# One seam pattern instead of thirteen in the feed-forward blocks of a two-layer encoder

## The chip, the cores and the metric

The kernel runs on one core of one Trainium2 chip. The metric is the device time of one launch in microseconds (us). The kernel before takes 1655.82 us in the median of three launches (1652.97 to 1657.56 us). Beside the launches there is one profiled execution of it, and all rows below are from that one.

## What is computed

The reference has two layers. In each layer the 256 tokens of 1024 channels go through a SwiGLU feed-forward network (FFN), a mixer of three attention-like branches, and a second FFN, each followed by a layer norm:

```python
def swiglu(x, w_in, w_out):
    gate, up = jnp.split(x @ w_in, 2, axis=-1)
    return (jax.nn.silu(gate) * up) @ w_out

for l in range(DEPTH):          # DEPTH = 2
    x = layer_norm(alpha * x + 0.5 * swiglu(x, w_ff1_in[l], w_ff1_out[l]), ln1_g[l], ln1_b[l])
    mix = hybrid_mixer(x, ...)
    x = layer_norm(alpha * x + mix, ln2_g[l], ln2_b[l])
    x = layer_norm(alpha * x + 0.5 * swiglu(x, w_ff2_in[l], w_ff2_out[l]), ln3_g[l], ln3_b[l])
```

So there are four FFNs, numbered 0 to 3 here. `w_in` is 1024 x 8192 (4096 gate and 4096 up channels) and `w_out` 4096 x 1024.

## The kernel before

Every float32 operand is split in two parts, `hi` and `lo`, and a product is made of three matmuls: hi x hi, hi x lo and lo x hi. ScalarE makes `hi` (line 90) and VectorE makes `lo` (line 91) of each weight tile of 128 x 1024, which the SyncE queue loads into a ring of three `raw` buffers; `hi` and `lo` have five buffers each.

An FFN works through 32 units of 128 hidden channels (loop in `ffn`, line 291). For one unit, `wide` (line 224) makes gate and up: 2 outputs x 8 slices of the input channels x 3 products = 48 matmuls of 256 columns. They all go through `mm` (line 191) and stand in the profile as line 198. This text calls them *input matmuls*, and writes w for one. After every second unit, `block` (line 203) makes the share of the output that the two units before the newest two give: 2 units x 2 halves of the tokens x 3 products x 2 halves of the output = 24 matmuls of 512 columns, which accumulate over the whole FFN in four PSUM tiles `acc` and stand as line 219. These are *output matmuls*, B for one. A *seam* is the passage from a block's output matmuls to the next unit's input matmuls. TensorE's stream in an FFN is thus, over and over, 24 B and 96 w: one *period*. An FFN has 13 blocks; the last is followed by 192 w, and then `finish` (line 240, matmuls of line 238) adds the last six units with their own weights.

The kernel before doesn't pass every seam in the same way. It keeps back the last few B of a block and puts them between the first w of the next unit. `block` puts them into `self.held`, each with the number of w after which it is due; `mm` counts the w in `self.done` and issues what is due (line 221 in the profile). Which B are kept back is a matter of the seam's *form*, an entry of the table at line 113:

```python
FORMS = ((), (2, 2), (1, 1), (3, 3), (1,), (2,), (3,), (2, 2, 2), (2, 2, 2, 2), (3,) * 6, (3, 6), "first", "rows")
```

The form (2, 2) keeps back two B and issues both after two w; (3, 6) issues one after three w and one after six; () keeps back none. "first" keeps back none but halves the first w into two matmuls of 128 columns (line 195), and "rows" halves the last B into two of 256 columns (line 217). Block j of FFN number f takes entry (j + 3 f) modulo 13, so each FFN passes through all 13 forms once, each time at another place. A seam is where the form's name applies: the form of block j shapes the end of that block and the start of the run of w behind it.

The instructions are laid out by a scheduler which keeps the order within an engine mostly as written. At the start of FFN 1, 2 and 3 it mixes the first block with the layer norm's transposes and the first three units, so that this block stands in pieces. The other 49 seams (13 in FFN 0, 12 in each of the others) stand as written.

Of the kernel before, what the change touches and what calls it, by code (L numbers as in the profile page):

```python
# [77 lines left out]
class Ring:  # L78
    def __init__(self, nc, pool):
        self.nc = nc  # L80
        self.pool = pool
# [28 lines left out]
PGT = ("vv", "vv", "vg")  # L110
PBR = ("vv", "vv", "vg")
ORDER = "K0 G4 B0 K1 G5 C0 K2 B1 K3 G7 k V0 G8 G6 V1 C1 G9 v i s G10 B2 C2 G11 G0 B3 G1 Z0 G2 Z1 G3 p R1 R2 R0"
FORMS = ((), (2, 2), (1, 1), (3, 3), (1,), (2,), (3,), (2, 2, 2), (2, 2, 2, 2), (3,) * 6, (3, 6), "first", "rows")


class Build:
    def __init__(self, nc, tc, pool, psum, dram, a):
        self.nc, self.tc, self.pool, self.psum, self.a = nc, tc, pool, psum, a
        self.ring = Ring(nc, pool)
        self.held, self.done, self.halves, self.nffn = [], 0, False, 0  # L120
        self.con = pool.tile([128, NCONST], F32, name="con")
        self.sums = pool.tile([128, NSUM], F32R, name="sums")
        self.nh = pool.tile([128, 16], F32, name="nh")
        nc.vector.memset(self.nh, -0.5)
        self.en = pool.tile([128, 8], F32, name="en")
        nc.vector.memset(self.en, float(np.e))
        self.dram = [dram.tile([8, 128, 16], F32, tag=f"d{i}", name=f"d{i}") for i in range(3)]
        self.ident = self.con[:, C_ID:C_ID + 128]
        self.xx = pool.tile([128, 8, 2, S], F32R, name="xhl")
        self.xh, self.xl = self.xx[:, :, 0], self.xx[:, :, 1]  # L130
        self.xs = [[x[:, k] for k in range(8)] for x in (self.xh, self.xl)]
        self.x = pool.tile([128, 2, D], F32, name="x")
# [52 lines left out]
    def mm3(self, out, wh, wl, xh, xl, start, stop):  # L185
        mm = self.mm
        mm(out, wh, xh, start=start, stop=False)
        mm(out, wh, xl, start=False, stop=False)
        mm(out, wl, xh, start=False, stop=stop)

    def mm(self, out, w, x, start, stop):
        mm = self.nc.tensor.matmul
        if self.halves:
            for c in (slice(0, 128), slice(128, 256)):
                mm(out[:, c], w, x[:, c], start=start and c.start == 0, stop=stop)
            self.halves = False
        else:
            mm(out, w, x, start=start, stop=stop)  # L198
        self.done += 1
        while self.held and self.held[0][0] <= self.done:  # L200
            self.held.pop(0)[1]()

    def block(self, acc, gs, ws, start, form):
        mm = self.nc.tensor.matmul
        todo = []
        for i, (g, w) in enumerate(zip(gs, ws)):
            for t in range(2):
                c = slice(t * 128, t * 128 + 128)
                for p, (x, y) in enumerate(((g[0], w[0]), (g[0], w[1]), (g[1], w[0]))):
                    for h in range(2):  # L210
                        todo.append((acc[t][h], x[:, c], y[:, h * 512:h * 512 + 512], start and i == 0 and p == 0))
        after = form if isinstance(form, tuple) else ()
        n = len(todo) - len(after)
        for q, (o, x, y, st) in enumerate(todo[:n]):
            if form == "rows" and q == n - 1:
                for d in (slice(0, 256), slice(256, 512)):
                    mm(o[:, d], x, y[:, d], start=st, stop=False)
            else:
                mm(o, x, y, start=st, stop=False)  # L219
        self.done = 0  # L220
        self.held = [(a, lambda o=o, x=x, y=y, st=st: mm(o, x, y, start=st, stop=False)) for a, (o, x, y, st) in zip(after, todo[n:])]  # L221
        self.halves = form == "first"

    def wide(self, out, w, xh, xl, nk):
        n = 0
# [25 lines left out]
    def ffn(self, wi, wo, lnp, first, last):  # L251
        nc = self.nc
        if not first:
            lng = self.load_ln(lnp)
        acc = None
        g = []

        def gate(gg, gate, up):
            s = self.tl(list(gg.shape), "cv")
            nc.scalar.activation(out=s, in_=gate, func=AF.Silu)  # L260
            nc.vector.tensor_tensor(out=gg, in0=s, in1=up, op=ALU.mult)  # L261

        n0 = 2 if first else NFIRST
        if first:
            ps = self.first(wi)
            for u in range(2):
                gg = self.tl([128, S], "th")
                gate(gg, ps[2 * u], ps[2 * u + 1])
                t = self.tl([128, 2, S], "g", F32R)
                self.split(t[:, 0], t[:, 1], gg)  # L270
                g.append((t[:, 0], t[:, 1]))
        else:
            tags = (OTHER + (RING,) * 4)[:2 * n0]
            ws, ps = [], []
            for u in range(n0):
                ws.append(self.ring.chunk(wi[u], tags=tags[2 * u:2 * u + 2], engs=self.engs(PFF[2 * u:2 * u + 2])))
                ps.append(self.ps([128, 2, S], "acc" if u < 2 else "mm"))
                g.append(self.tl([128, 2, S], "g", F32R))
            for t in range(2):
                c = slice(t * 128, t * 128 + 128)  # L280
                for u in range(n0):
                    for k in range(8):
                        hi, lo = [w[:, (k % 4) * S:(k % 4) * S + S] for w in ws[u][k // 4]]
                        self.mm3r(ps[u][:, t], self.xs[0][k][:, c], self.xs[1][k][:, c], hi, lo, k == 0, k == 7)
                    gg = self.tl([128, 128], "th")
                    gate(gg, ps[u][:, t, 0:128], ps[u][:, t, 128:256])
                    tp = self.ps([128, 128], "sm")
                    nc.tensor.transpose(tp, gg, self.ident)
                    self.split(g[u][:, 0, c], g[u][:, 1, c], tp)
            g = [(t[:, 0], t[:, 1]) for t in g]  # L290
        for u in range(n0, 32):
            w = self.ring.chunk(wi[u])
            if first and u in (6, 10):
                with self.tc.issue_after(self.ring.last.ins):
                    if u == 6:
                        self.second()
                    else:
                        lng = self.load_ln(lnp, nc.sync)
            gg = self.tl([128, S], "th")
            ps = self.ps([128, 2, S], ("mm", "sm")[u // 2 % 2])  # L300
            self.wide(ps, w, self.xs[0], self.xs[1], 8)
            gate(gg, ps[:, 0], ps[:, 1])
            t = self.tl([128, 2, S], "g", F32R)
            self.split(t[:, 0], t[:, 1], gg)
            g.append((t[:, 0], t[:, 1]))
            j = u // 2 - 1
            if u % 2 == 1 and u >= 3 and 2 * j < 32 - NLAST:
                if acc is None:
                    acc = [[self.ps([128, 512], "acc") for h in range(2)] for t in range(2)]
                self.block(acc, g[2 * j:2 * j + 2], self.ring.chunk(wo[j]), j == 0, FORMS[(j + 3 * self.nffn) % len(FORMS)])  # L310
        self.nffn += 1
        tags = (EXTRA + (RING,) * 4)[:NLAST]
        ws = []
        for n in range(NLAST // 2):
            ws += self.ring.chunk(wo[16 - NLAST // 2 + n], tags=tags[2 * n:2 * n + 2])
        self.finish(acc, g[32 - NLAST:], ws, 0.5, lng, last)
# [51 lines left out]
    def mixer(self, l):  # L368
# [472 lines left out]
        for j in range(4):  # L841
# [6 lines left out]
            st=2, mv=2, ve=2, rs=2, nm=4, sum=4, rsum=4, es=4)  # L848
# [78 lines left out]
```

## Time and profile before

| | |
|---|---|
| three launches, median | 1655.82 us (1652.97 to 1657.56) |
| profiled execution, its own time | 1655.71 us |
| its span, first to last instruction | 1653.9 us |
| mean granted TensorE clock | 0.997 of full speed |
| TensorE (PE) busy | 1630.6 us, 99% of the span |
| VectorE (DVE) busy | 1046.1 us, 63% |
| ScalarE (ACT) busy | 791.4 us, 48% |
| PE's share of the chain that ended last | 91%; lines 198: 56%, 219: 16%, 238: 8%, 221: 1% |

The profile gives each engine's busy time, the instructions behind it by source line, and what ended each wait. A matmul's busy time overlaps its neighbours' (the end is modelled), so how fast matmuls follow each other is read from their number in a stretch of time and not from the mean duration of one. In a table of windows a number in brackets counts every instruction that touches the window, so two or three at the edges come on top of those that start in it.

### The profile page before, as it was taken

The numbers are of one execution on the slowest core, as the hardware profiler recorded it, in microseconds if no ns is written. First come the engines' busy times: TensorE is split into PE (matmuls) and PEld (weight loads), VectorE is DVE, ScalarE is ACT, GpSimd is POOL, SyncE is SP. The second block draws the span as 40 slices with busy tenths as digits, with TensorE's granted clock in tenths as the row PEclk, the third lists the DMA queues.
The fourth block names the chain that finished last, engine by engine and source line by source line (L and its number), as shares of the span: only waits on it lengthen the run. The fifth ranks groups of instructions, "written<-read, shape, count | busy, mean of one in ns | idle before, by whom it ended". The sixth has DMA issues, their size and how long they took to land.

```text
span 1653.9 us, 29281 instructions
## 1 busy us (share of the span) xinstructions
PE 1630.6 (99%) x12246; PEld 1521.2 (92%) x12246; DVE 1046.1 (63%) x1580; ACT 791.4 (48%) x1297; POOL 175.1 (11%) x145
## 2 busy tenths in 40 slices
PE   9999999999999999999999999999999999999998
PEld 7999998999889899999999999989988889999997
DVE  6555555889669755555655555667886696555555
ACT  5444453675444444444444444536754444444442
POOL 0000001123014400000110000011320152000000
PEclk9999999999999999999999999999999999999999
DMA  8655553634335555555555555535353355555552
GB/s 319 226 198 181 198 203 120 222 141 154 129 131 195 182 201 183 199 181 201 184 199 185 197 183 199 198 137 208 139 164 120 108 202 180 204 199 185 195 185 77
DMA packets 52341, 298.28 MB, mean 180 GB/s; under 512 B 11600, under 2 KB 13520, under 8 KB 18672
## 3 DMA queue, kind: packets, MB, share of 16 engines
q1 hardware_dynamic: 50208, 289.39, 48.9%
q0 software_dynamic: 2000, 7.01, 1.2%
q8 instruction: 96, 1.57, 0.4%
q14 instruction: 37, 0.30, 0.1%
HBM read 294.94 MB, written 1.44 MB: 179 GB/s over the span
## 4 chain that ended last, share of the span: by engine, by line
PE 91%; DVE 5%; DMA 1%; ACT 1%; issue 1%; SPq 0%; POOL 0%; DVEq 0%; ACTq 0%; POOLq 0%
PE mm L198 36%; PE sm L198 20%; PE acc L219 16%; PE acc L238 8%; DVE lo L91 2%; PE acc L221 1%; DMA raw<-w1i 1%; PE acc L322 1%; PE acc L320 1%; PE acc L704 1%; PE acc L321 1%; PE sm L534 1%; PE sm L585 1%; ACT hi L90 1%; PE sm L526 1%; DVE cv L478 1%
## 5 line engine op out<-in xcount | busy, mean ns | idle before, releaser
L91 DVE TENSOR_TENSOR lo<-raw,hi 128x1024 fp32r<-128x1024 f32 (+1 forms) x498 | 617.4, 1245 | 481.7 <-ACT hi L90 480.8
L90 ACT ACTIVATE hi<-raw 128x1024 fp32r<-128x1024 f32 (+1 forms) x542 | 564.2, 1050 | 656.8 <-PE mm L198 196.0
L198 PE MATMUL mm<-xhl,hi 128*128 128x256 f32 x3486 | 619.6, 280 | 0.0
L198 PEld LDWEIGHTS mm<-xhl,hi 128*128 128x128 f32 x3486 | 533.8, 188 | 9.0 <-issue 5.8
L198 PE MATMUL mm<-xhl,lo 128*128 128x256 f32 x1744 | 487.7, 280 | 0.0
L198 PE MATMUL sm<-xhl,hi 128*128 128x256 f32 x1950 | 341.5, 279 | 0.8 <-ACT hi L90 0.8
L198 PEld LDWEIGHTS mm<-xhl,lo 128*128 128x128 f32 x1744 | 330.0, 189 | 3.7 <-issue 2.4
L198 PEld LDWEIGHTS sm<-xhl,hi 128*128 128x128 f32 x1950 | 298.4, 188 | 3.4 <-ACT hi L90 1.0
L198 PE MATMUL sm<-xhl,lo 128*128 128x256 f32 x976 | 271.9, 279 | 0.8 <-DVE lo L91 0.8
L219 PE MATMUL acc<-hi,g 128*128 128x512 f32 x752 | 209.5, 390 | 0.0
L198 PEld LDWEIGHTS sm<-xhl,lo 128*128 128x128 f32 x976 | 184.6, 189 | 1.4 <-DVE lo L91 1.0
L219 PEld LDWEIGHTS acc<-hi,g 128*128 128x128 f32 x752 | 137.0, 188 | 25.1
L91 POOL TENSOR_TENSOR lo<-raw,hi 128x1024 fp32r<-128x1024 f32 (+1 forms) x44 | 103.8, 2373 | 368.8 <-DVE g L147 243.8
L219 PE MATMUL acc<-lo,g 128*128 128x512 f32 x396 | 122.4, 389 | 0.0
L343 POOL TENSOR_TENSOR rs<-ve,nh 128x1 f32<-128x1 f32 x12 | 11.8, 982 | 775.0 <-DVE ve L341 775.0
L238 PE MATMUL acc<-hi,g 128*128 128x512 f32 x320 | 92.8, 392 | 0.0
L219 PEld LDWEIGHTS acc<-lo,g 128*128 128x128 f32 x396 | 74.3, 188 | 15.8
L238 PEld LDWEIGHTS acc<-hi,g 128*128 128x128 f32 x320 | 59.3, 188 | 13.3 <-DVE g L149 0.7
L238 PE MATMUL acc<-lo,g 128*128 128x512 f32 x160 | 54.6, 390 | 0.0
L147 DVE TENSOR_TENSOR g<-th,g 128x256 fp32r<-128x256 f32 x119 | 51.0, 429 | 2.1 <-ACT g L145 1.9
L145 ACT ACTIVATE g<-th 128x256 fp32r<-128x256 f32 x119 | 47.8, 402 | 5.7 <-DVE th L261 5.7
L478 DVE SCALAR_TENSOR_TENSOR cv<-cin,par,cv 128x256 f32<-128x256 f32 x72 | 41.7, 625 | 0.2
(239 smaller groups left out, 1543.5 us busy)
## 6 DMA issues: line engine op xcount, KB each, us to landing
raw<-w2i SPq DMA_DIRECT2D x64, 1024.0 KB, 4.8
raw<-w1i SPq DMA_DIRECT2D x62, 1024.0 KB, 4.8
raw<-w1o SPq DMA_DIRECT2D x32, 1024.0 KB, 4.8
raw<-w2o SPq DMA_DIRECT2D x32, 1024.0 KB, 4.8
raw<-wg SPq DMA_DIRECT2D x28, 1024.0 KB, 4.8
raw<-wgt SPq DMA_DIRECT2D x24, 1024.0 KB, 4.8
raw<-wbr SPq DMA_DIRECT2D x12, 1024.0 KB, 4.8
raw<-wout SPq DMA_DIRECT2D x8, 1024.0 KB, 4.9
```

The source lines that it names most:

```text
L90: nc.scalar.activation(out=hi, in_=raw, func=AF.Copy)
L91: (eng or nc.vector).tensor_tensor(out=lo, in0=raw, in1=hi.bitcast(F32), op=ALU.subtract)
L145: nc.scalar.activation(out=hi, in_=src, func=AF.Copy, scale=scale)
L147: nc.vector.tensor_tensor(out=lo, in0=src, in1=hi.bitcast(F32), op=ALU.subtract)
L198: mm(out, w, x, start=start, stop=stop)
L219: mm(o, x, y, start=st, stop=False)
L221: self.held = [(a, lambda o=o, x=x, y=y, st=st: mm(o, x, y, start=st, stop=False)) for a, (o, x, y, st) in zip(after, todo[n:])]
L238: mm(acc[h], x[:, c], y[:, h * n:h * n + n], start=start and i == 0, stop=stop and i == 2)
L320: mm(out, xh, wh, start=start, stop=False)
L321: mm(out, xh, wl, start=False, stop=False)
L322: mm(out, xl, wh, start=False, stop=stop)
L478: V.scalar_tensor_tensor(out=cv, in0=cin[:, q:q + S], scalar=w[:, q:q + 1], in1=cv, op0=ALU.mult, op1=ALU.add)
```

## The change

The table of forms goes away, and with it the two halving forms and the counter of w. `block` now always keeps back its last two B, and `mm` issues whatever is held right after the next w. That is the form (1, 1) at every seam: 22 B, one w, two B, and then the other w.

```diff
-FORMS = ((), (2, 2), (1, 1), (3, 3), (1,), (2,), (3,), (2, 2, 2), (2, 2, 2, 2), (3,) * 6, (3, 6), "first", "rows")
...
     def mm(self, out, w, x, start, stop):
-        mm = self.nc.tensor.matmul
-        if self.halves:
-            for c in (slice(0, 128), slice(128, 256)):
-                mm(out[:, c], w, x[:, c], start=start and c.start == 0, stop=stop)
-            self.halves = False
-        else:
-            mm(out, w, x, start=start, stop=stop)
-        self.done += 1
-        while self.held and self.held[0][0] <= self.done:
-            self.held.pop(0)[1]()
+        self.nc.tensor.matmul(out, w, x, start=start, stop=stop)
+        held, self.held = self.held, []
+        for h in held:
+            self.nc.tensor.matmul(*h[:3], start=h[3], stop=False)
...
-        after = form if isinstance(form, tuple) else ()
-        n = len(todo) - len(after)
...
+        self.held = todo[-2:]
+        for o, x, y, st in todo[:-2]:
+            self.nc.tensor.matmul(o, x, y, start=st, stop=False)
```

Of the 49 seams that stand as written, four have the form (1, 1) already, one in each FFN; the other 45 change. The pieces of the first blocks of FFN 1, 2 and 3 stand as they did. On VectorE, ScalarE, GpSimd and SyncE the instructions stand in the same order as before, all of them; TensorE loses eight instructions (the second halves) of 11,847 and keeps all others.

TensorE at the first seam of FFN 0, before (form ()): `acc<-hi,g` and `acc<-lo,g` are output matmuls, `xhl,hi` and `xhl,lo` input matmuls of the next unit.

```order
L219 MATMUL acc<-lo,g 128x512 x2
L219 MATMUL acc<-hi,g 128x512 x4
L219 MATMUL acc<-lo,g 128x512 x2
L219 MATMUL acc<-hi,g 128x512 x2
L198 MATMUL mm<-xhl,hi 128x256 x2
L198 MATMUL mm<-xhl,lo 128x256
```

TensorE at the same place after; line 192 is the issue of the held matmuls, line 189 an input matmul.

```order
L204 MATMUL acc<-lo,g 128x512 x2
L204 MATMUL acc<-hi,g 128x512 x4
L204 MATMUL acc<-lo,g 128x512 x2
L189 MATMUL mm<-xhl,hi 128x256
L192 MATMUL acc<-hi,g 128x512 x2
L189 MATMUL mm<-xhl,hi 128x256
L189 MATMUL mm<-xhl,lo 128x256
```

The last two output matmuls moved behind the first input matmul; nothing else moved.

TensorE at the tenth seam of FFN 0, before (form (3,) * 6).

```order
L219 MATMUL acc<-hi,g 128x512 x4
L219 MATMUL acc<-lo,g 128x512 x2
L219 MATMUL acc<-hi,g 128x512 x2
L198 MATMUL sm<-xhl,hi 128x256 x2
L198 MATMUL sm<-xhl,lo 128x256
L221 MATMUL acc<-hi,g 128x512 x2
L221 MATMUL acc<-lo,g 128x512 x2
L221 MATMUL acc<-hi,g 128x512 x2
L198 MATMUL sm<-xhl,hi 128x256 x2
```

TensorE at the same place after.

```order
L204 MATMUL acc<-hi,g 128x512 x4
L204 MATMUL acc<-lo,g 128x512 x2
L189 MATMUL sm<-xhl,hi 128x256
L192 MATMUL acc<-hi,g 128x512 x2
L189 MATMUL sm<-xhl,hi 128x256
L189 MATMUL sm<-xhl,lo 128x256
```

Six output matmuls stood behind three input matmuls; now two stand behind one.

TensorE at the first seam of FFN 1 that stands as written (block 1, form (1,)), before.

```order
L219 MATMUL acc<-hi,g 128x512 x4
L219 MATMUL acc<-lo,g 128x512 x2
L219 MATMUL acc<-hi,g 128x512
L198 MATMUL sm<-xhl,hi 128x256
L221 MATMUL acc<-hi,g 128x512
L198 MATMUL sm<-xhl,hi 128x256
L198 MATMUL sm<-xhl,lo 128x256
```

TensorE at the same place after.

```order
L204 MATMUL acc<-hi,g 128x512 x4
L204 MATMUL acc<-lo,g 128x512 x2
L189 MATMUL sm<-xhl,hi 128x256
L192 MATMUL acc<-hi,g 128x512 x2
L189 MATMUL sm<-xhl,hi 128x256
L189 MATMUL sm<-xhl,lo 128x256
```

One more output matmul moved behind the first input matmul.

## Rows read from the trace of the kernel before

**Rows 1.** The page's first part: engine, busy us, share of the span, instructions.

```profile
PE   1630.6 (99%) x12246; PEld 1521.2 (92%) x12246; DVE 1046.1 (63%) x1580; ACT 791.4 (48%) x1297; POOL 175.1 (11%) x145
```

**Rows 2.** Windows of PE, line 198, one behind each seam of FFN 0, in order.

```profile
core 0: us, PE busy (x), PEclk, DMA share, GB/s
36.80:46.80 10.00, 10.00 (x87) 1.00 0.91 359
54.00:64.00 10.00, 10.00 (x91) 1.00 0.57 210
70.20:80.20 10.00, 10.00 (x90) 1.00 0.72 261
87.00:97.00 10.00, 10.00 (x87) 1.00 0.56 206
103.50:113.50 10.00, 10.00 (x88) 1.00 0.58 211
120.30:130.30 10.00, 10.00 (x87) 1.00 0.55 211
137.10:147.10 10.00, 10.00 (x87) 1.00 0.60 212
154.00:164.00 10.00, 10.00 (x91) 1.00 0.60 211
170.70:180.70 10.00, 10.00 (x87) 1.00 0.53 205
187.40:197.40 10.00, 10.00 (x88) 1.00 0.56 208
204.20:214.20 10.00, 10.00 (x87) 1.00 0.53 208
220.50:230.50 10.00, 10.00 (x91) 1.00 0.59 211
237.00:247.00 10.00, 10.00 (x91) 1.00 0.70 250
```

**Rows 3.** Windows of PE, line 198, in FFN 1, 2 and 3.

```profile
590.50:598.50 8.00, 8.00 (x70) 1.00 0.79 305
788.00:798.00 10.00, 10.00 (x90) 1.00 0.70 256
860.50:868.50 8.00, 8.00 (x73) 1.00 0.71 264
875.00:885.00 10.00, 10.00 (x91) 1.00 0.61 210
1007.60:1017.60 10.00, 10.00 (x91) 1.00 0.61 211
1507.70:1517.70 10.00, 10.00 (x91) 1.00 0.61 211
```

**Rows 4.** Windows of PE, all lines, from a block's first B to a later block's.

```profile
31.19:258.06 226.87, 226.87 (x1661) 1.00 0.58 210
598.76:808.91 210.15, 210.15 (x1540) 1.00 0.55 196
868.93:1079.47 210.54, 210.54 (x1541) 1.00 0.55 195
1418.91:1629.50 210.59, 210.59 (x1540) 1.00 0.53 185
64.30:80.67 16.37, 16.37 (x123) 1.00 0.74 257
97.43:114.19 16.76, 16.76 (x123) 1.00 0.52 189
781.67:808.91 27.24, 27.24 (x218) 1.00 0.65 234
```

**Rows 5.** Groups by line, FFN 0: count, busy us, mean ns, idle before, who ended it.

```profile
L91 DVE TENSOR_TENSOR lo<-raw,hi 128x1024 fp32r<-128x1024 f32 (+1 forms) x87 | 105.4, 1216 | 102.9 <-ACT hi L90 102.9
L90 ACT ACTIVATE hi<-raw 128x1024 fp32r<-128x1024 f32 (+1 forms) x86 | 90.2, 1053 | 117.2 <-issue 37.5 <-PE sm L198 30.2 <-PE mm L198 27.4
```

More of the change, by code (lines that the diff above doesn't have):

```diff
@@ L119, in __init__ @@
         self.ring = Ring(nc, pool)
-        self.held, self.done, self.halves, self.nffn = [], 0, False, 0
+        self.held = []
         self.con = pool.tile([128, NCONST], F32, name="con")
@@ L191, in mm, with block @@
     def mm(self, out, w, x, start, stop):
-        mm = self.nc.tensor.matmul
-        if self.halves:
-            for c in (slice(0, 128), slice(128, 256)):
-                mm(out[:, c], w, x[:, c], start=start and c.start == 0, stop=stop)
-            self.halves = False
-        else:
-            mm(out, w, x, start=start, stop=stop)
-        self.done += 1
-        while self.held and self.held[0][0] <= self.done:
-            self.held.pop(0)[1]()
-    def block(self, acc, gs, ws, start, form):
-        mm = self.nc.tensor.matmul
+        self.nc.tensor.matmul(out, w, x, start=start, stop=stop)
+        held, self.held = self.held, []
+        for h in held:
+            self.nc.tensor.matmul(*h[:3], start=h[3], stop=False)
+    def block(self, acc, gs, ws, start):
         todo = []
@@ L211, in block @@
                         todo.append((acc[t][h], x[:, c], y[:, h * 512:h * 512 + 512], start and i == 0 and p == 0))
-        after = form if isinstance(form, tuple) else ()
-        n = len(todo) - len(after)
[L214 to L222, printed above, removed]
+        self.held = todo[-2:]
+        for o, x, y, st in todo[:-2]:
+            self.nc.tensor.matmul(o, x, y, start=st, stop=False)
     def wide(self, out, w, xh, xl, nk):
@@ L309, in ffn @@
                     acc = [[self.ps([128, 512], "acc") for h in range(2)] for t in range(2)]
-                self.block(acc, g[2 * j:2 * j + 2], self.ring.chunk(wo[j]), j == 0, FORMS[(j + 3 * self.nffn) % len(FORMS)])
-        self.nffn += 1
+                self.block(acc, g[2 * j:2 * j + 2], self.ring.chunk(wo[j]), j == 0)
         tags = (EXTRA + (RING,) * 4)[:NLAST]
```

## The prediction

> **What bounds the kernel now.** The page comes first: TensorE is busy 99% of the span, VectorE 63%, ScalarE 48% [rows 1]. Such a kernel gets faster only if TensorE has less to do or does the same at a closer pace, and the busy share can't show the second, since matmuls overlap in it. So the next view is a table of windows of equal length, one behind each seam of FFN 0, in which the input matmuls are counted [rows 2]. The reader is to see two values there and nothing between: 90 or 91 matmuls of 256 columns in 10 us, or 87 or 88. The granted clock is 1.00 in both, the engine is busy for the whole 10.00 us in both. So there are two paces of the same instruction, about 4% apart, each held for the whole run between two blocks.
>
> The 13 rows of [rows 2] stand behind the 13 forms of the table in order. The close pace (90, 91) follows (2, 2), (1, 1), (2, 2, 2), "first" and "rows"; the wide pace (87, 88) follows (), (3, 3), (1,), (2,), (3,), (2, 2, 2, 2), (3,) * 6 and (3, 6). Hence the reading on which the forecast rests: the form of a seam sets the pace of the run behind it.
>
> A place in the FFN could do that as well as a form, and [rows 3] tells the two apart, because the forms are shifted by three from one FFN to the next. Form (1, 1) stands behind block 2 of FFN 0, 12 of FFN 1, 9 of FFN 2 and 6 of FFN 3, and the windows behind them (third row of [rows 2]; those from 788.00, 1007.60 and 1507.70 in [rows 3]) count 90, 90, 91 and 91: close, four of four. Does the pace ahead of a block matter for the pace behind it? Form (2, 2, 2) answers: in FFN 0 it follows a wide run (87, window from 137.10) and a close run comes (91); in FFN 2 it follows a close run (73 in 8 us, from 860.50, where the wide pace gives 70, as from 590.50) and a close run comes again (91, from 875.00). It was the same behind either.
>
> **The change part by part.** Prices first, by windows from one block's first output matmul to a later one's [rows 4]. A period of 24 B and 96 w takes 16.37 us with form (1, 1), 64.30 to 80.67, and 16.76 us with form (1,), 97.43 to 114.19: 0.39 us for the pace. The long run behind the last block takes 27.24 us with form (1, 1), 781.67 to 808.91.
>
> The 45 seams that change. I replace every period by one of form (1, 1). FFN 0 holds 12 periods and a long run: 12 x 16.37 + 27.24 = 223.68 us for 226.87, a gain of 3.19. The others hold, from the first whole block on, 11 periods and a long run: 11 x 16.37 + 27.24 = 207.31. FFN 1 takes 210.15 (gain 2.84), FFN 2 210.54 (3.23), FFN 3 210.59 (3.28). The sum is 12.54 us. A second way to it: by the list above 8, 7, 7 and 7 of the runs in these stretches are wide, 29 in all, of which two (the ends of FFN 2 and 3) are long runs of 192 w and count about double, so 31 x 0.39 = 12.1; the rest is a little more than the halved matmuls cost.
>
> The eight matmuls less (second halves of "first" and "rows") are in these sums. Alone they are small either way: the same columns are still streamed.
>
> The bookkeeping in Python issues nothing. The order on the other engines is unchanged, so no DMA, no conversion and no queue is passed by another; no wait is added.
>
> What is late next. The weights for 24 w (one tile of 1024 columns, 8 slices by 3 products) are converted by ScalarE in 1.053 us and by VectorE in 1.216 us, one tile behind the other on separate engines [rows 5]. At the close pace TensorE needs 24 x 10/88 = 2.7 us for them (88 being 91 less the three at a window's edges). Of VectorE's idle time all ends with ScalarE, and half of ScalarE's with TensorE, which hands back a buffer. The suppliers wait for the consumer, so a pace 2.4% closer by period (16.37 for 16.76) finds them ready, and I cost this at nothing. If that cover were gone, the price would be bounded by what is gained, 0.39 us per period. The DMA share in the close runs is 0.57 to 0.72, so loads have room as well.
>
> Two things the trace doesn't show. One is form (1, 1) behind a wide run: all four of its seams follow a close one, and with the change the first whole blocks of FFN 1 and 3 do follow a wide one (70 in 8 us from 590.50 for FFN 1; FFN 3 begins with the same pieces). At best it costs 16.37, at worst it keeps 16.76; I take 16.37, for (2, 2) and (2, 2, 2) both turn wide into close. The other is what the mixers do between the FFNs: their order is unchanged and the finish with its matmuls of 512 columns lies before them, so I take 0.
>
> A rule that speaks against the gain. What the rows show: at a granted clock of 1.00, 87 or 91 matmuls of one shape in 10 us [rows 2]. The Trainium skill, page "TensorE: Matmul & The Clock Gate", section "Back-to-back issue gap", gives the warm distance of isolated matmuls by the columns alone, N/2.4 + 2.5 ns, thus 109 ns for 256 columns wherever they stand. By that rule the order can't matter and the sum would be 0; by the rows it is 12.5 us. The trace disagrees, with one shape at two paces, and I go by the trace.
>
> The sum: 1655.71 us of the profiled execution (its span of 1653.9 and 1.8 around it) less 12.5 is 1643.2. The median of the launches is 1655.82, the same within 0.1.
>
> **The rivals.** *The seam hands on the pace that it meets.* Form (1, 1) would keep a close run close and a wide run wide. For it: all four of its seams have close on both sides. Against it: its neighbour (2, 2) always turns wide to close, and (2, 2, 2) gave one outcome behind either pace. FFN 0 and 2 begin close and would gain 3.19 + 3.23; FFN 1 and 3 would be wide throughout: 11 x 16.76 and a long run of 27.24 + 2 x 0.39 = 28.02 (estimate) make 212.38, a loss of 2.23 and 1.79. Time: 1655.7 - 6.42 + 4.02 = 1653.3.
>
> *The pace belongs to the place or to the instruction stream as a whole*, and forms only happen to go with it, or the supply of weights can't hold the close pace for 160 us on end. Nothing is gained: 1655.7. Against it: the four places of (1, 1) in [rows 2, 3], and the end of FFN 0, from 214 on, where the close pace holds for two periods and a long run with TensorE busy throughout.
>
> *A run of 95 w spoils the next seam.* With (1, 1) a block is met after exactly 95 w from the last held B. In the trace every seam behind such a run of 95 is one that ends wide: (3, 3) behind (1, 1), (2,) behind (1,). If that run and not the form made them wide, the change would put every seam behind the first of each FFN in that position, and this decides at the second seam of FFN 0, at 47.6 us. FFN 0: 16.37 + 11 x 16.76 + 28.02 = 228.75, a loss of 1.88; the others 16.37 + 10 x 16.76 + 28.02 = 211.99, losses of 1.84, 1.45 and 1.40. Sum 6.6: 1662.3, slower by 0.4%. Against it: the other six wide forms follow runs of 96, 94 or 93 w, so no special run is needed to make a seam wide, and all forms which put three w ahead of the held B are wide whatever is ahead.
>
> **How the numbers follow.** The forecast has 0.83, the seam that hands on 0.05, place or supply 0.05, the run of 95 w 0.07. A measurement of this kernel can tell a change from none at about 0.3%, which is 5.0 us: the forecast is faster (-0.76%), the second and third are within it, the fourth is slower. So faster 0.83, same 0.10, slower 0.07. Around the forecast lies what the launches differ by, 2.3 us to either side; above it some seams could fail, and one whole FFN that stays wide costs about 5. The range of 1639.5 to 1649.0 holds that and leaves out the three rivals.
>
> **What would show it.** In the changed profile, windows of 10 us behind each seam of all four FFNs should count 90 or 91 input matmuls (line 189); each period should take 16.37 us; the four stretches of [rows 4] should take 223.7, 207.3, 207.3 and 207.3 us. The first whole blocks of FFN 1 and 3 test the untried case: if 87 follow there and from then on, the seam hands the pace on; if 91 follow in the first period and 87 in all others, the run of 95 w was it. If TensorE shows idle time before input matmuls, ended by line 91 or 90, the supply has become the bound. The forecast is wrong if the two paces occur with form (1, 1) in any mixture.

## The result and the profile after

The changed kernel takes 1646.07 us in the median of four launches (1645.89 to 1646.29), the kernel before 1655.01 us in four launches beside them (1652.97 to 1657.56). The ratio is 0.9945, 95% interval [0.9928, 0.9962]: 0.55% faster. Forecast were 1643.2 us, a ratio of 0.9924, within a range of 1639.5 to 1649.0. Measured again (below, run "same") the ratio was 0.9925 [0.9912, 0.9937].

The page of the changed kernel answers to [rows 1]: TensorE is as busy by share as before, with 9.7 us less of it (x counts the profile's records: eight fewer, the second halves).

```profile
PE 1620.9 (99%) x12238; PEld 1511.0 (92%) x12238; DVE 1045.7 (64%) x1580; ACT 791.5 (48%) x1297; POOL 175.3 (11%) x145
```

Windows of TensorE, input matmuls alone (now line 189), answer to [rows 2, 3]: behind the first and the fifth seam of FFN 0, then behind the first whole block of FFN 1 and of FFN 3.

```profile
core 0: us, PE busy (x), PEclk, DMA share, GB/s
38.00:48.00 10.00, 10.00 (x91) 1.00 0.93 359
103.50:113.50 10.00, 10.00 (x91) 1.00 0.61 211
602.50:612.50 10.00, 10.00 (x90) 1.00 0.59 211
1418.80:1428.80 10.00, 10.00 (x90) 1.00 0.57 211
```

All are close: 90 or 91 matmuls where a wide run has 87. By the mean distance from start to start, all 49 runs behind whole blocks are close (113.4 ns for the 117.8 of a wide run). Windows of all of TensorE's matmuls, from a block's first output matmul to a later one's, answer to [rows 4]: the four FFN stretches, a period, and the period that follows a wide run.

```profile
32.07:255.71 223.64, 223.64 (x1658) 1.00 0.60 214
596.58:803.89 207.31, 207.31 (x1538) 1.00 0.56 199
864.48:1071.75 207.27, 207.27 (x1539) 1.00 0.56 198
1412.65:1619.96 207.31, 207.31 (x1538) 1.00 0.52 188
32.07:48.44 16.37, 16.37 (x123) 1.00 0.93 344
596.58:612.98 16.40, 16.40 (x123) 1.00 0.55 194
```

The forecast for the four was 223.7 and three times 207.3 us; they came out within 0.05 us. Together they gave 3.23 + 2.84 + 3.27 + 3.28 = 12.62 us. The span fell by 1653.9 - 1644.5 = 9.4 us, so 3.2 us went back elsewhere. The same view of what lies between the FFN stretches shows where: first the kernel before, then the changed one, each with the start, the first mixer, the layer norm between FFN 1 and 2, the second mixer and the end.

```profile
0.00:31.19 31.19, 27.32 (x197) 1.00 0.85 301
258.06:598.76 340.70, 336.02 (x2652) 0.99 0.45 160
808.91:868.93 60.02, 58.16 (x409) 1.00 0.47 175
1079.47:1418.91 339.44, 334.43 (x2652) 1.00 0.45 159
1629.50:1653.90 24.40, 16.48 (x74) 0.88 0.12 44
```

```profile
0.00:32.07 32.07, 27.76 (x196) 1.00 0.82 281
255.71:596.58 340.87, 336.18 (x2653) 0.99 0.45 160
803.89:864.48 60.59, 58.74 (x408) 1.00 0.47 172
1071.75:1412.65 340.90, 336.20 (x2652) 0.99 0.45 158
1619.96:1644.50 24.54, 16.50 (x74) 0.94 0.12 44
```

Start +0.88, first mixer +0.17, norm +0.57, second mixer +1.46, end +0.14: 3.22 us, though every engine has the same instructions in the same order there. Three rows of each trace name the two larger causes: a run of 21 input matmuls in the second mixer, and the runs of 55 and of 87 beside the pieces of FFN 2's first block. Before:

```profile
1215.76:1218.25 2.49, 2.49 (x23) 1.00 0.02 7
852.34:858.59 6.25, 6.25 (x56) 1.00 0.45 170
859.06:868.93 9.87, 9.87 (x89) 1.00 0.57 214
```

After:

```profile
1207.97:1212.08 4.11, 4.11 (x22) 0.58 0.02 4
847.31:853.78 6.47, 6.47 (x56) 1.00 0.45 165
854.24:864.48 10.24, 10.24 (x88) 1.00 0.54 206
```

The run of 21 took 4.11 us for 2.49 at a granted clock of 0.58 for 1.00: TensorE ran most of it at the lower of its two levels, 1.2 instead of 2.4 GHz. What it did just before was alike in both executions: it had waited for VectorE, as the timeline shows (start, duration, and in brackets the idle time before); the kernel before:

```profile
1214.91 0.48 PE L533 MATMUL sm<-kc,qk 64*128 64x128 f32 x2 [1.63 <-DVE qk L600]
```

and the changed one:

```profile
1207.12 0.48 PE L514 MATMUL sm<-kc,qk 64*128 64x128 f32 x2 [1.56 <-DVE qk L581]
```

The runs of 55 and 87 took 0.22 and 0.37 us more at a granted clock of 1.00: they are at the wide pace now and were at the close one before.

### The profile page after: what moved, and what is told of

It is laid out like the page before. It is cut to its first block, busy times and chain, and to the rows that moved or that the text cites. A ratio compares the mean times of both kernels' runs of the same rounds, so it can differ in the third digit from the quotient of the medians.

```text
span 1644.5 us, 29265 instructions
## 1 busy us (share of the span) xinstructions
PE 1620.9 (99%) x12238; PEld 1511.0 (92%) x12238; DVE 1045.7 (64%) x1580; ACT 791.5 (48%) x1297; POOL 175.3 (11%) x145
## 4 chain that ended last, share of the span: by engine, by line
PE 93%; DVE 4%; ACT 1%; DMA 1%; issue 0%; SPq 0%; POOL 0%; DVEq 0%; ACTq 0%; POOLq 0%
PE mm L189 37%; PE sm L189 20%; PE acc L204 16%; PE acc L220 8%; DVE lo L91 2%; PE acc L192 1%; PE acc L301 1%; PE acc L303 1%; PE acc L685 1%; PE sm L515 1%; PE acc L302 1%; PE sm L566 1%; PE sm L507 1%; PE sm L514 1%; ACT hi L90 1%; DVE cv L459 1%
## 5 line engine op out<-in xcount | busy, mean ns | idle before, releaser
L204 PE MATMUL acc<-hi,g 128*128 128x512 f32 x728 | 200.4, 391 | 0.0
L204 PEld LDWEIGHTS acc<-hi,g 128*128 128x128 f32 x728 | 132.4, 188 | 24.2
L204 PE MATMUL acc<-lo,g 128*128 128x512 f32 x416 | 128.4, 390 | 0.0
L204 PEld LDWEIGHTS acc<-lo,g 128*128 128x128 f32 x416 | 78.1, 188 | 16.8
L220 PE MATMUL acc<-hi,g 128*128 128x512 f32 x320 | 92.8, 392 | 0.0
L220 PEld LDWEIGHTS acc<-hi,g 128*128 128x128 f32 x320 | 59.3, 188 | 13.3 <-ACT g L142 0.8
L220 PE MATMUL acc<-lo,g 128*128 128x512 f32 x160 | 54.7, 391 | 0.0
```

The costliest lines, as they stand in the source:

```text
L204: self.nc.tensor.matmul(o, x, y, start=st, stop=False)
L220: mm(acc[h], x[:, c], y[:, h * n:h * n + n], start=start and i == 0, stop=stop and i == 2)
```

## The experiments

**The change unaltered (run "again").**

The edit is none: the changed kernel runs as it is.

> The changed kernel once more, unchanged, for a second profile. In its first profile the four FFN stretches gave back 12.6 us as forecast, but 3.2 us were lost elsewhere: 1.1 us in the first 192 input matmuls, 1.6 us in a run of 21 input matmuls of the second mixer at half the granted clock, 1.0 us in the runs next to the pieces of the first blocks of FFN 1 to 3. Theory A (these vary from one execution to the next and are not the change's): the four FFN stretches are again 223.6, 207.3, 207.3, 207.3 us within 0.1, while the start, the run of 21 or the pieces come out differently by 0.3 us or more somewhere. Theory B (the change moved them for good): all of them are again as in the first profile, within 0.1 us.

1647.46 us, one launch. The stretches took 223.67, 207.31, 207.26 and 207.31 us; the run of 21 in the second mixer came out slow again:

```profile
33.51:257.18 223.67, 223.67 (x1658) 1.00 0.58 210
1209.39:1213.47 4.08, 4.08 (x22) 0.58 0.02 4
```

The start moved by another 1.4 us (33.51 for 32.07), as theory A has it. There too it is the clock: in this profile the granted clock is 0.58 from 21.58 to 25.60 us, with 23 matmuls in 4.02 us, where the first profile has 1.00 from 22.04 to 25.60 us, with 33 in 3.56 us. The second mixer and the pieces of FFN 2 (runs of 55 and 87 wide again) did as theory B has it. Undecided after this.

**No output matmul held back (run "none_all").** In the kernel before:

```diff
-                self.block(acc, ..., FORMS[(j + 3 * self.nffn) % len(FORMS)])
+                self.block(acc, ..., ())
```

> Form () at every seam: no output matmul is held back. Theory A (the form sets the pace): every run is wide, a period takes 16.76 us and the long run 28.1, FFN stretches 229.2 and three times 212.4 us, in all 21 us above the changed kernel: 1667 us, ratio to the kernel before 1.007. Theory B (the seam hands on the pace it meets, or the place sets it): FFN 0 enters close and would stay close, or the stretches come out between the two kernels: 1646 to 1656 us, ratio 0.994 to 1.000.

1664.67 us, ratio to the kernel before 1.005 [1.0033, 1.0067]. All 49 runs behind whole blocks are wide (of the three behind the pieces, the one in FFN 2 is close); FFN 0:

```profile
31.55:260.58 229.03, 229.03 (x1658) 1.00 0.58 208
```

FFN 0 enters this stretch close (113.3 ns over the 40 input matmuls ahead of its first block) and is wide from its first seam on, which refutes theory B. Between () and (1, 1) at every seam lie 229.03 - 223.64 = 5.4 us in FFN 0, with the same matmuls. The other three stretches took 212.31, 212.28 and 212.31 us, so that all four differ from the changed kernel by 20.4 us, as theory A forecast to within 1 us; the median came out 2.3 us under its 1667 us.

**Form (2, 2) at every seam (run "two_all").**

```diff
-                self.block(acc, ..., FORMS[(j + 3 * self.nffn) % len(FORMS)])
+                self.block(acc, ..., (2, 2))
```

> Form (2, 2) at every seam. Theory A (the form sets the pace, and what counts is a pair of output matmuls behind one or two input matmuls): every run is close, a period takes 16.35 us, 0.016 us less than with (1, 1), so 1645.3 us, ratio to the kernel before 0.994. Theory B (a run of 94 or 95 input matmuls ahead of the block, or the one matmul of the pair of equal weights, makes (1, 1) close only): at least some runs are wide and the time is above 1648 us.

1645.36 us (1642.75 to 1651.87, six launches), ratio 0.9934 [0.9915, 0.9954]; all 49 runs behind whole blocks are close:

```profile
32.95:256.59 223.64, 223.64 (x1658) 1.00 0.58 212
49.31:65.68 16.37, 16.37 (x123) 1.00 0.55 196
```

Theory A, but for the period: 16.37 and not 16.35 us. The 16.35 of the kernel before (47.95 to 64.30 us) belonged to periods that began behind a wide run; this is not the form's. It comes back here in the one period of FFN 2 that begins behind a wide run (865.32 to 881.67 us).

**New forms (run "forms_new").**

```diff
-FORMS = ((), (2, 2), (1, 1), ...)
+FORMS = ((1, 1, 1), (), (1, 1, 1, 1), (4, 4), (5, 5), (6, 6), (1, 2), (49, 49), (48, 48), (3, 3, 3), (1, 1), (7, 7), (1, 1, 49, 49))
+STEP = (1, 2, 5, 7)
...
-                FORMS[(j + 3 * self.nffn) % len(FORMS)]
+                FORMS[(j * STEP[self.nffn] + 3 * self.nffn) % len(FORMS)]
```

> Thirteen forms of which eleven were never run, in four different orders over the FFNs: (1,1,1), (), (1,1,1,1), (4,4), (5,5), (6,6), (1,2), (49,49), (48,48), (3,3,3), (1,1), (7,7), (1,1,49,49). Read from the trace as a table, not from the time. Theory A (a pair counts where it stands inside a triple hi x hi, hi x lo, lo x hi, wherever in the run): close (113.3 ns) behind (4,4), (5,5), (7,7), (1,1,1), (1,1); wide (117.8 ns) behind (), (6,6), (3,3,3), (1,1,1,1), (1,2), (48,48); (49,49) wide up to the pair and close behind it; each form the same in all four FFNs. Theory B (a pair counts only within two input matmuls of the block): (4,4), (5,5), (7,7), (49,49) wide as well. Theory C (the pace ahead of the block matters): a form comes out differently in different FFNs.

Windows on the input matmuls in FFN 0: behind (1,1,1), (4,4), (5,5) and (6,6); then ahead of and behind the pair of (49,49).

```profile
37.50:47.50 10.00, 10.00 (x87) 1.00 0.81 319
88.00:98.00 10.00, 10.00 (x90) 1.00 0.59 206
104.30:114.30 10.00, 10.00 (x91) 1.00 0.60 211
121.00:131.00 10.00, 10.00 (x87) 1.00 0.56 205
153.20:158.20 5.00, 5.00 (x45) 1.00 0.62 213
159.30:164.30 5.00, 5.00 (x46) 1.00 0.42 143
```

Theory B and C fall: a pair switches the pace far from the block, after 49 input matmuls, and each form did the same in every order in which it stands at a whole block. Theory A holds but for (1,1,1), which is wide everywhere. In a 5 us window the two paces differ by two counts at most; as mean distance from start to start the trace has 117.8 ns ahead of the pair of (49,49) and 113.3 ns behind it (its first three left out).

**Another order of the three products (run "lo_first").** The table of forms is also replaced, as the expectation lists it, in the four orders of "forms_new".

```diff
-        mm(out, wh, xh, start=start, stop=False)
-        mm(out, wh, xl, start=False, stop=False)
-        mm(out, wl, xh, start=False, stop=stop)
+        mm(out, wl, xh, start=start, stop=False)
+        mm(out, wh, xh, start=False, stop=False)
+        mm(out, wh, xl, start=False, stop=stop)
```

> The three products of every input slice in another order: lo x hi first, then hi x hi and hi x lo (so the two matmuls with the same stationary tile are now the second and third of a triple), with the forms (), (1,1), (2,2), (3,3), (1,), (2,), (3,), (1,1,1), (2,2,2), (3,3,3), (4,4), (5,5), (6,6), in four orders over the FFNs. Read from the trace as a table. Theory A (what counts is which two input matmuls the pair comes between: beside a hi x hi to hi x lo or a hi x lo to lo x hi passage it makes the run close, between lo x hi and hi x hi it doesn't): now (2,2), (3,3), (5,5), (6,6) close and (1,1), (4,4) wide. Theory B (the number of input matmuls since the block, modulo 3, counts, whatever they hold): as before, (1,1), (2,2), (4,4), (5,5) close and (3,3), (6,6) wide.

Behind (1,1), (2,2), (3,3), (5,5) and (6,6) of FFN 0:

```profile
54.00:64.00 10.00, 10.00 (x91) 1.00 0.60 210
70.70:80.70 10.00, 10.00 (x91) 1.00 0.66 257
87.30:97.30 10.00, 10.00 (x88) 1.00 0.55 206
220.40:230.40 10.00, 10.00 (x90) 1.00 0.60 211
237.00:247.00 10.00, 10.00 (x87) 1.00 0.71 251
```

Theory A, mine, is refuted and B holds: which products stand beside the pair doesn't matter, the number of input matmuls modulo 3 does. (The launch took 1675.22 us. Its two mixers take 8.2 and 11.0 us more than in the kernel before, with longer waits of TensorE for VectorE; it says nothing on the seams.)

**One, two and three output matmuls in the middle of a run (run "forms_far").** The orders over the FFNs are those of "forms_new".

```diff
-FORMS = ((), (2, 2), (1, 1), ...)
+FORMS = ((1, 1, 48, 48), (1, 1, 48), (1, 1, 49), (1, 1, 50), (1, 1, 48, 48, 48), (1, 1, 49, 49, 49), (1, 1, 50, 50, 50), (50, 50), (51, 51), (49, 49, 49), (50, 50, 50), (49,), (50,))
```

> Forms that put one, two or three output matmuls into the middle of a run, behind 48 to 51 input matmuls, either into a run that a pair after the first input matmul has made close, (1,1,48,48), (1,1,48), (1,1,49), (1,1,50), (1,1,48,48,48), (1,1,49,49,49), (1,1,50,50,50), or into a wide run, (50,50), (51,51), (49,49,49), (50,50,50), (49,), (50,). Read from the trace as a table. Theory A (a pair inside a triple makes the run close, a pair between two triples hands on the pace that it meets): (50,50) and (50,50,50) wide then close, (51,51) and (49,49,49) wide throughout, (1,1,48,48) close throughout; a single one hands on what it meets. Theory B (any group but a pair inside a triple sets the wide pace): all of the (1,1,...) forms are close up to 48 and wide behind it.

Ahead of and behind the single one of (1,1,48):

```profile
55.50:60.50 5.00, 5.00 (x46) 1.00 0.62 210
61.00:66.00 5.00, 5.00 (x45) 1.00 0.39 123
```

By the distances from start to start this is 113.3 ns ahead (its first three left out) and 117.8 behind. A pair hands on the close pace, (1,1,48,48) staying close throughout, as theory A says. A single one, or three, in a close run make it wide, in all FFNs, as B says of them; theory A's guess on single ones was wrong. The table has all groups that were held back in the eleven profiles of this study and have a run of seven or more w behind them, paces as mean distance of starts, with n the number of w since the last B. Where n is under 7, the run ahead is too short for a pace and is put down as wide, as a run behind a whole block is with form (). Left out are the pairs behind the first block of FFN 2, one in each profile, which stand 55 to 96 w behind a block in pieces and to which the last part of this section returns.

| group of B | ahead | n modulo 3 | behind | cases |
|---|---|---|---|---|
| one | wide or close | any | wide | 50 of 50 |
| two | wide | 1 or 2 | close | 374 of 374 |
| two | wide | 0 | wide | 24 of 24 |
| two | close | 0 or 2 (48, 47) | close | 8 of 8 |
| three | wide | 2 | close | 12 of 12 |
| three | wide | 0 or 1 | wide | 17 of 17 |
| three | close | any (47 to 49) | wide | 11 of 11 |
| four, six | wide | 0, 1, 2 | wide | 11 of 11 |

**The first blocks' pieces (run "pieces").** The counting code of the kernel before, with

```diff
+                self.block(acc, ..., (1, 1) if j or first else (19, 19) if self.nffn % 2 else (10, 10))
```

> The changed kernel, but the two output matmuls held back from the first block of FFN 1 and 3 are due after 19 input matmuls instead of 1, and those of FFN 2 after 10, so that they stand 3 (with 16 that the scheduler has drawn ahead) and 56 input matmuls behind the pieces ahead of them, inside a triple. Theory A (a pair inside a triple makes the run close): the runs of 77, 86 and 77 behind them count at the close pace, 1.0 to 1.1 us less in all (77 x 4.4 ns twice, 86 x 4.4 ns once) than the changed kernel on the same chip, if its three runs there are wide again. Theory B (the pieces are ruled by the waits beside them): no difference in the runs.

The runs of 77 stayed wide, in FFN 1 and FFN 3; the run of 86 in FFN 2 was close, but so were the 56 matmuls ahead of its pair. In FFN 1:

```profile
588.50:596.50 8.00, 8.00 (x70) 1.00 0.82 313
```

My theory failed again: the pair is inside a triple there (67 matmuls into the units), but three w behind the last B. The ratio to the kernel before is 0.9932 [0.9918, 0.9945], no better than the unaltered change beside it. Its run of 21 in the second mixer shows the other outcome, after a wait of 1.58 us:

```profile
1208.03:1210.50 2.47, 2.47 (x22) 1.00 0.03 7
```

**The change unaltered, on the same chip (run "same").**

The edit is none: the changed kernel runs as it is.

> The changed kernel unchanged, beside the one with the moved pieces, for the comparison on one chip and for a third profile. Theory A (start and clock vary by execution): ratio to the kernel before again 0.993 to 0.996; the FFN stretches 223.6 and three times 207.3 us; start and runs of 21 as they fall, the granted clock at half in those runs of 21 that take 4.1 us and at 1.00 in those that take 2.5 us. Theory B (a loss of 1.6 us in the second mixer belongs to the change): the run of 21 in the second mixer takes 4.1 us again, and never less in a profile of the changed kernel.

1643.16 us (1642.32 to 1644.69, five launches) against 1656.24, ratio 0.9925 [0.9912, 0.9937]. The FFN stretches are 223.65, 207.32, 207.28 and 207.32 us. Beside the pieces of FFN 2 the runs of 55 and 87 were close this time, with no edit:

```profile
1206.58:1210.20 3.62, 3.62 (x22) 0.66 0.02 5
846.47:852.73 6.26, 6.26 (x57) 1.00 0.46 170
853.19:863.06 9.87, 9.87 (x88) 1.00 0.57 214
```

So theory A holds for the pieces: their pace differs between executions of one program. The clock is less plain. In the second mixer all three profiles of the changed kernel show the fall (a granted clock below 1.00 over the run of 21), and so do "two_all" (0.58) and "pieces2" (0.66), which are close throughout; but "pieces", as close, shows none (2.5 us at 1.00). Among the kernels with wide runs "forms_new" shows it (0.58, 4.09 us), while the kernel before, "none_all" (2.5 us at 1.00) and "forms_far" don't. The same 21 matmuls in the first mixer fell in eight of these ten profiles, the kernel before (3.75 us) and "none_all" (3.69 us) among them, and not in "pieces" and here (2.58 us). So the fall doesn't belong to one order of the seams; whether the close pace makes it more frequent, and whether the rest is chance, is not shown.

**The pieces by the count (run "pieces2").** Against the run "pieces":

```diff
-                ... (1, 1) if j or first else (19, 19) if self.nffn % 2 else (10, 10))
+                ... (1, 1) if j or first else ((), (17, 17), (1, 1), (18, 18))[self.nffn])
```

> The changed kernel, but of the first block of FFN 1 the two held output matmuls are due after 17 input matmuls and of FFN 3 after 18, so that they stand one and two input matmuls behind the other six of that piece (in the run with the pieces moved by 19 they stood three behind, and the runs of 77 stayed wide). Two behind is the boundary of two triples there, one behind is inside a triple. Theory A (what counts is the number of input matmuls since the last output matmul, modulo 3: one or two make the run close): both runs, of 79 and of 78, close, 0.35 us less each than the changed kernel, 0.7 us in all, too little for the launches to tell. Theory B (the place in the triple counts): the run of 79 in FFN 1 close, the run of 78 in FFN 3 wide.

Windows behind the moved pairs in FFN 1 and FFN 3, then the same place of the changed kernel in FFN 1:

```profile
586.00:594.00 8.00, 8.00 (x73) 1.00 0.84 324
1401.00:1409.00 8.00, 8.00 (x73) 1.00 0.87 335
```

```profile
587.50:595.50 8.00, 8.00 (x70) 1.00 0.86 326
```

Both are close, so the count since the last B decides and not the place in the triple. The span of its profile, 1641.3 us, is the least of all; the launches (1644.22 us, ratio 0.9933 [0.992, 0.9947]) can't tell 0.7 us, as expected. No version here is shown to beat the change.

**What the weight loads show (all eleven profiles).** The traces hold one more sign of the pace, in the duration of TensorE's weight loads (PEld). First a wide run, "none_all", then the close run at the same place of the changed kernel, 70.5 to 81 us; the second number behind the bar is the mean duration in ns.

```profile
L198 PEld LDWEIGHTS mm<-xhl,hi 128*128 128x128 f32 x60 | 9.2, 188 | 0.0
L198 PEld LDWEIGHTS mm<-xhl,lo 128*128 128x128 f32 x30 | 5.8, 192 | 0.0
```

```profile
L189 PEld LDWEIGHTS mm<-xhl,hi 128*128 128x128 f32 x62 | 9.3, 188 | 0.0
L189 PEld LDWEIGHTS mm<-xhl,lo 128*128 128x128 f32 x32 | 6.0, 188 | 0.0
```

In the wide run every third load takes 192 ns and the others 188; in the close run all take 188. Of the runs of 40 or more w behind a B, all 230 wide ones have such a long load in every three, and none of the 414 close ones has. Behind a whole block it is the third load, whichever product that is (lo x hi here, hi x lo in "lo_first"), and this gives the count modulo 3 a plainer form. Of the pairs behind at least seven w of a wide run, all 12 that stand directly behind a long load leave the run wide, and all 14 that stand elsewhere turn it close. That takes in the pairs that the table leaves out: in FFN 2 of the changed kernel's first profile, of "again" and of "two_all" a pair 55 w behind the last B left a wide run wide, and in "forms_far" one 96 w behind turned it close, both against the count and both as the place of the long load has it. The long load goes with the wide pace; that it causes it is not shown.

## Why the prediction was right, and where it was off

**The reading of the two paces** held in full: a table of windows in the old trace, in which each form stands three or four times, gave the four FFN stretches to 0.05 us. The untried case, form (1, 1) behind a wide run, became close in FFN 1, 2 and 3 of the first profile; its first period took 16.40 us in FFN 1 and 3 and 16.36 in FFN 2 for the 16.37 that I took.

**What is late next** held: TensorE stays busy for the whole of all four stretches.

**The terms set to 0** are what failed: "what the mixers do between the FFNs", set to 0 because their order is unchanged, and the start and the pieces of the first blocks, which the sum doesn't name. In the first profile they cost 3.2 us, which is more than the miss of 2.9 us in the median. The order was indeed unchanged, but the order doesn't fix their time. The pieces' share, 0.2 + 0.6 + 0.2 us, is a matter of the pace; 1.6 us is the clock in the second mixer and 0.4 us that in the first; the start is 0.9 us and the end 0.1; other places in the mixers gave back 0.8. The profile that the sum starts from held one fall of the clock in the mixers, the first profile after the change two.

All of these differ between executions of one program: the second measurement came to 1643.16 us, with the forecast at 1643.2. The mean granted clock goes with it, 0.996 or 0.997 in the four launches of the first measurement and 0.997 to 0.999 in the five of the second. That the second median meets the forecast to 0.1 us is therefore luck, as those five lie between 1642.32 and 1644.69 us. My range had taken in the launches' own spread, and it needed that.

**The rivals.** The run of 95 is refuted by every period behind the first. Place or supply is refuted by "none_all" and "two_all", same places, same weights, two paces. The seam that hands on its pace is wrong for (1, 1) and yet right for another pair: behind a number of w divisible by 3, or directly behind a long weight load, a pair does just that. My reading of the old table by form was a list without a rule; it was enough for the sum, and the rule that I first put in its place, the place inside a triple, fell with the run "pieces".

**The Trainium skill's rule**, page "TensorE: Matmul & The Clock Gate", section "Back-to-back issue gap", gives a distance of N/2.4 + 2.5 ns for isolated matmuls by the columns alone, 109 ns for 256 columns as an estimate by that formula. The traces disagree: they show 113.3 and 117.8 ns for one shape by order alone, so the forecast of no gain that I worked out from it is refuted here. The Trainium skill gives the formula for isolated matmuls and not for a stream of weight loads and matmuls, which is what runs here.

**What stays open.** Why a pair that doesn't stand behind a long load makes the following matmuls close, and one or four B make them wide, I can't say: the long load marks the wide pace, but no view shows what holds a matmul back 4.4 ns. The forms "first" and "rows", close in the kernel before, hold back no pair and are in no rule here. Nor is it shown why the clock falls after the same wait in some executions and not in others; no run removed that wait. And what sets the pace behind the pieces of FFN 2, among transposes, close in some executions of one program and wide in others, is not shown.

## What to carry to other kernels

Where one engine is busy 99% of the time, count its instructions in windows of equal length, stage by stage: two counts for one shape at one clock are a gain that the busy share hides. Order alone can set such a pace, and it is worth testing a dozen orders within one launch, each at several places, before choosing one; the trace then forecasts the change to hundredths of a us where the engine never waits. Leave room in the range for the stages with waits, where executions of one program differ by up to 2.8 us of span here (1645.6 and 1642.8 us), about a quarter of what this change is worth.

## What the runs showed of the hardware that was not expected

Matmuls of 256 columns follow each other at 113.3 or 117.8 ns at a granted clock of 1.00, and the pace lasts through a run, up to 192 matmuls here, until output matmuls of 512 columns come between. Two of these make a wide run close unless they stand directly behind a long weight load (14 of 14, and 12 of 12 that leave it wide); one or four make it wide, as tabled above. In a wide run every third weight load takes 192 ns for 188, in a close run none. After a wait of 1.56 to 1.63 us TensorE's granted clock stood at 0.58 or 0.66 over the next 21 matmuls in the second mixer of some profiles (3.7 to 4.1 us for the run) and at 1.00 in that of others (2.5 us), with one order of the mixer's instructions.
